# Neighbourhood attention: values for four heads side by side instead of two, loaded four heads at a time

## The chip, the cores and the metric

One core of a Trainium2 chip runs the whole kernel in one launch. The metric is the device time in microseconds (us) of one execution. The core has TensorE (PE in the profile, its weight loads PEld), VectorE (DVE), ScalarE (ACT), GpSimd (POOL) and SyncE (SP). SP and POOL also issue the DMA transfers of this kernel.

## The reference, cut to what matters

The kernel computes one layer of a hybrid backbone: 512 latent tokens (8 rows of a 64-column grid) and 256 context tokens, width 1024, float32. Only the neighbourhood attention changes. It has 16 heads of dimension 32; every query attends to an 8 x 16 window of the grid and to all 256 context tokens:

```python
def one_row(r):
    ...
    s_lat = jnp.einsum("bqhd,bkhd->bhqk", qb, kb, preferred_element_type=jnp.float32) * scale + bias
    s_lat = jnp.where(band_mask, s_lat, -jnp.inf)
    s_ctx = jnp.einsum("bqhd,bkhd->bhqk", qb, k_ctx, preferred_element_type=jnp.float32) * scale
    p = jax.nn.softmax(jnp.concatenate([s_lat, s_ctx], -1), -1).astype(v.dtype)
    n_lat = kh * GRID_W
    return (jnp.einsum("bhqk,bkhd->bqhd", p[..., :n_lat], vb)
            + jnp.einsum("bhqk,bkhd->bqhd", p[..., n_lat:], v_ctx))
```

Around it: one input projection, a gated position-mixing branch, the merge of both branches, an output projection, and a mixture of 64 experts whose weights (1 MB a tile) fill the second half of the run.

## The kernel before

**Stages, in order of time.** Normalisation and projections (to about 225 us), the first half of the gating branch (`phase_u`), then a stage that weaves two streams: `up_a` and `gates` are projections with 512-column matmuls (tile `mmp`, lines 135 to 137, three matmuls for one float32 product), and `na()` is the neighbourhood attention, advanced by `weave` some 1.5 steps after each half of a weight piece. Then `up_b`, `w_out`, the router, and the experts.

**The attention.** A unit is one head on one quarter g of the grid's columns: 128 queries against 256 latent keys (the quarter's 32-column window of all 8 rows) and 256 context keys. With 16 heads and 4 quarters that makes the 64 units that `units` lists. The tiles `q4` and `k4` hold the operands of a pair of heads `hp`; `hh` is a head's place among four. Each unit is a chain over the engines: two score matmuls (`stp`, L836 and L837), minimum and bias on DVE (L840, L841), two exponentials on ACT (L844, L845), the normalisation on DVE (L869 to L871, which completes `npr`), four transposes on PE (`tpp`, L874), and a copy to `npt` (L876, on DVE and ACT by turns).

**The products with the values** (`pvp`, L859) follow a few units later. The stationary operand is a slab of values of one head, 128 keys x 32 columns of the tile `vw`, so a matmul fills 32 of the array's 128 columns and writes 32 partitions of the PSUM tile `pv`; the moving operand is `npt` (128 columns). Heads that write different groups of 32 partitions use different columns of the array. Before, two heads are worked at a time: for each of 4 slabs of keys, one matmul for each of the two heads. In the trace each such float32 matmul is two instructions, so a batch of 2 heads x 4 slabs is 16 of them.

**Loads.** `fetch` reads a pair's `q4` and `k4` with 8 DMAs on POOL's queue (L790); two buffers each. `na_start` reads all values of all heads into one `vw` tile with 34 DMAs (L802, L804) before the first unit. `nab` reads the bias of one pair and one type of quarter on SP's queue, into the four buffers of the tag `bc`. Weight pieces (`raw`, L124) and, later, expert weights (`rw`, L1215) are also on SP's queue.

**Order.** In this stage a scheduler sets the order on each engine from the program's order and its own costs; an engine then runs its instructions strictly in that order.

Of the kernel before, what the change touches and what calls it, by code (L numbers as in the profile page):

```python
# [7 lines left out]
F32 = mybir.dt.float32  # L8
F32R = mybir.dt.float32r
# [8 lines left out]
P = 128  # L18
D = 1024
S = 512  # L20
C = 256
T = S + C
# [5 lines left out]
GBASE = (0, 8, 24, 32)  # L28
GTYPE = (0, 1, 1, 2)
# [62 lines left out]
class Kern:  # L92
# [49 lines left out]
    def run(self):  # L142
        tc, nc, A = self.tc, self.nc, self.A
        with ExitStack() as es:
# [25 lines left out]
            self.zn = zn_.__enter__()  # L170
            na = self.na()
            next(na)
            self.phase_u()
            self.weave(self.stream(self.up_a() + self.gates(0) + self.gates(1)), na, self.WV, 68)
            zn_.__exit__(None, None, None)
            mid_ = tc.tile_pool(name="mid", bufs=1, side="right", reuse_waits="tile")
# [606 lines left out]
    def na_loads(self, hp):  # L783

        nc, zn = self.nc, self.zn
        q4 = zn.tile([P, 2, S], F32R, name="q4", tag="q4", bufs=2)
        k4 = zn.tile([P, 2, T], F32R, name="k4", tag="k4", bufs=2)
        for gi in range(4):
            for t, src, part, n in ((q4, self.qdr, gi // 2, S), (k4, self.kdr, gi % 2, T)):
                nc.gpsimd.dma_start(t[gi * 32:gi * 32 + 32], src[part, hp * 64:hp * 64 + 64, :]  # L790
                                    .rearrange("(h d) t -> d h t", d=32))
        return q4, k4

    def na_start(self):
        nc, zn = self.nc, self.zn
        self.vw = zn.tile([P, 10, 512], F32, name="vw")
        v = self.vdr
        for g in range(4):
            for c in range(2):
                for r in range(4):  # L800
                    t0 = (4 * c + r) * 64 + GBASE[g]
                    nc.gpsimd.dma_start(self.vw[r * 32:r * 32 + 32, g * 2 + c, :], v[t0:t0 + 32, 64:576])  # L802
        for c in range(2):
            nc.gpsimd.dma_start(self.vw[:, 8 + c, :], v[S + c * P:S + c * P + P, 64:576])  # L804
        self.obhi, self.oblo = [], []

    def na(self):

        nc, zn = self.nc, self.zn
        units = [(hp, g, hh) for hp in range(8) for g in range(4) for hh in (hp % 2 * 2, hp % 2 * 2 + 1)]  # L810
        qk, bias, pr, pts = {}, {}, {}, {}

        def fetch(hp):
            if hp < 8:
                qk[hp] = self.na_loads(hp)

        def nab(i):
            if i < 24:
                hp = i // 3
                bias[i] = self.p1.tile([P, 2, 256], F32, name="nab", tag="bc", bufs=4)  # L820
                nc.sync.dma_start(bias[i], self.A["nab"][i % 3, hp // 2, :, hp % 2 * 512:hp % 2 * 512 + 512]
                                  .rearrange("p (h k) -> p h k", h=2))

        fetch(0), fetch(1)
        self.na_start()
        yield
        nab(0), nab(1)
        for n in range(len(units) + 4):
            if n < len(units):
                hp, g, hh = units[n]  # L830
                q4, k4 = qk[hp]
                bt = bias[hp * 3 + GTYPE[g]]
                ps = self.st_tile()
                q = q4[:, hh % 2, g * P:g * P + P]
                kw = k4[:, hh % 2, :S].rearrange("p (r c) -> p r c", c=64)[:, :, GBASE[g]:GBASE[g] + 32]
                nc.tensor.matmul(ps[:, 256:], lhsT=q, rhs=k4[:, hh % 2, S:], start=True, stop=True)  # L836
                nc.tensor.matmul(ps[:, :256], lhsT=q, rhs=kw, start=True, stop=True)  # L837
                m = zn.tile([P, 8], F32, name="nm", tag="nm", bufs=4)
                sb = zn.tile([P, 256], F32, name="nsb", tag="nsb", bufs=2)
                nc.vector.tensor_reduce(out=m[:, 0:1], in_=ps[:, 256:], axis=AX.X, op=ALU.min)  # L840
                nc.vector.tensor_tensor_reduce(out=sb, in0=ps[:, :256], in1=bt[:, hh % 2, :], scale=-1.0,  # L841
                                               scalar=m[:, 0:1], op0=ALU.add, op1=ALU.min, accum_out=m[:, 1:2])
                pr[n] = zn.tile([P, 512], F32, name="npr", tag="npr", bufs=2), m
                nc.scalar.activation(pr[n][0][:, :256], sb, AF.Exp, bias=m[:, 1:2], scale=-1.0, accum_out=m[:, 2:3])  # L844
                nc.scalar.activation(pr[n][0][:, 256:], ps[:, 256:], AF.Exp, bias=m[:, 1:2], scale=-1.0, accum_out=m[:, 3:4])  # L845
                if hh % 2 and g != 1:
                    nab(hp * 3 + GTYPE[g] + 2)
                if hh % 2 and g == 3:
                    fetch(hp + 2)
            yield  # L850
            if n >= 3 and n % 2 and n - 3 < len(units):
                hp, g, hh = units[n - 3]
                if hh + g == 0:
                    pv = self.pv_tile()
                for c in range(4):
                    vi = g * 2 + c if c < 2 else 6 + c
                    for i in range(2):
                        h = hp * 2 + i
                        nc.tensor.matmul(pv[(hh + i) * 32:(hh + i) * 32 + 32, g * P:g * P + P],  # L859
                                         lhsT=self.vw[:, vi, h * 32:h * 32 + 32],  # L860
                                         rhs=pts[n - 3 + i][:, c * P:c * P + P], start=c == 0, stop=c == 3)
                for i in range(2):
                    pts.pop(n - 3 + i)
                if hp % 2 and g == 3:
                    self.na_done(pv)
            if 0 < n <= len(units):
                hh = units[n - 1][2]
                p, m = pr.pop(n - 1)
                nc.vector.tensor_tensor(m[:, 4:5], m[:, 2:3], m[:, 3:4], op=ALU.add)  # L869
                nc.vector.reciprocal(m[:, 5:6], m[:, 4:5])  # L870
                nc.vector.tensor_scalar(p, p, m[:, 5:6], None, op0=ALU.mult)  # L871
                tp = self.tp_tile()
                for i in range(4):
                    nc.tensor.transpose(tp[:, i * P:i * P + P], p[:, i * P:i * P + P], self.ident)  # L874
                pt = zn.tile([P, 512], F32, name="npt", tag="npt", bufs=5)
                (nc.scalar.copy if hh % 2 else nc.vector.tensor_copy)(pt, tp)  # L876
                pts[n - 1] = pt
# [877 lines left out]
```

## Time and profile before

| what | value |
|---|---|
| time, median of 3 runs | 1319.64 us (1318.62 to 1322.22) |
| the profiled execution's own time | 1315.69 us |
| its span, first to last instruction | 1313.8 us |
| PE busy | 1199.2 us (91%) |
| PE weight loads busy | 835.5 us (64%) |
| DVE busy | 831.2 us (63%) |
| ACT busy | 612.5 us (47%) |
| POOL busy | 397.7 us (30%) |

Matmuls are pipelined: the profile gives a matmul its whole passage through the array, so a busy PE says that something was always in the array, not that it took work at its best rate. What a matmul costs its successors is the distance from its start to the start of the next one. Attention runs from about 285 to 495 us of the span.

### The profile page before, as it was taken

What the parts mean: (1) busy time and instruction counts of PE and PEld (TensorE: products, weight loads), DVE (VectorE), ACT (ScalarE), POOL (GpSimd) and SP (SyncE); (2) the same over time, 40 slices, a digit from 0 to 9 for tenths busy, and PEclk for the clock granted to TensorE, in tenths of its full rate; (3) what the DMA queues carried; (4) which work ended last, traced back from release to release, by engine and by line L of the source; (5) the groups of instructions that cost most, each with busy time, mean ns of one, the idle gap of its engine ahead of it and who ended that gap; (6) DMA issues with size and microseconds to landing.
All of it is one profiled execution on the core that took longest, in us unless ns stands there. A gap on an engine that the chain in (4) does not pass through costs nothing.

```text
span 1313.8 us, 18428 instructions
## 1 busy us (share of the span) xinstructions
PE 1199.2 (91%) x6305; PEld 835.5 (64%) x6305; DVE 831.2 (63%) x1470; ACT 612.5 (47%) x1086; POOL 397.7 (30%) x380
## 2 busy tenths in 40 slices
PE   6999999999999999989899899888797898898990
PEld 4875787887777778877643445655464565555660
DVE  4535356756777765675944635767676876766763
ACT  4411155345555554334523434565465566665641
POOL 2400111511211100042644534534253434443422
PEclk8999999999999999988999999989798999999996
DMA  9999553944674636584899999999999999999984
GB/s 326 323 308 296 161 175 86 224 148 113 143 163 113 151 113 214 182 320 159 265 309 365 305 355 366 349 344 332 348 358 359 347 367 363 364 376 363 365 297 145
DMA packets 107465, 353.46 MB, mean 269 GB/s; under 512 B 14081, under 2 KB 41322, under 8 KB 82410
## 3 DMA queue, kind: packets, MB, share of 16 engines
q1 hardware_dynamic: 82634, 289.86, 61.6%
q0 software_dynamic: 24272, 60.82, 19.5%
q10 hardware_dynamic: 464, 1.59, 0.3%
q8 instruction: 51, 0.84, 0.3%
q14 instruction: 44, 0.36, 0.1%
HBM read 323.45 MB, written 39.53 MB: 276 GB/s over the span
## 4 chain that ended last, share of the span: by engine, by line
DMA 30%; PE 15%; DVE 5%; issue 3%; ACT 1%; POOL 1%; SPq 0%; POOLq 0%; DVEq 0%; ACTq 0%
DMA rw<-in_w_exp_dram 27%; PE py L1340 5%; PE pg L1294 5%; DVE gq L1267 2%; PE pg L1281 2%; PE xt L1387 1%; DMA accb<-y,rows 1%; DMA xg<-h2d,half 1%; DMA accd<-y,ix 1%; DVE oh L1180 1%; PE mmp L137 1%; DMA accb<-y,ix 1%; ACT gq L1265 1%; PE mmp L136 1%; PE mmp L135 1%
## 5 line engine op out<-in xcount | busy, mean ns | idle before, releaser
L1294 PE MATMUL pg<-gq,xx 128*128 128x512 f32 x1136 | 331.6, 428 | 0.8 <-DVE gq L1267 0.8
L1267 DVE TENSOR_TENSOR gq<-rw,gq 128x1024 fp32r<-128x1024 f32 x210 | 264.1, 1270 | 82.5 <-ACT gq L1265 81.4
L1294 PEld LDWEIGHTS pg<-gq,xx 128*128 128x128 f32 x1136 | 207.0, 192 | 78.7 <-issue 30.2
L1265 ACT CAST gq<-rw 128x1024 fp32r<-128x1024 f32 x216 | 222.0, 1047 | 64.7 <-DMA rw<-in_w_exp_dram 42.1
L1340 PE MATMUL py<-rw,hT 128*128 128x512 f32 (+1 forms) x560 | 216.9, 625 | 37.2 <-DMA rw<-in_w_exp_dram 30.0
L1353 POOL TENSOR_TENSOR y<-y,gf 128x512 f32<-128x512 f32 x52 | 75.1, 1445 | 270.6 <-ACT y L1352 270.5
L1340 PEld LDWEIGHTS py<-rw,hT 128*128 128x128 f32 (+1 forms) x560 | 74.7, 171 | 125.0 <-issue 109.5
L118 ACT CAST whi<-raw 128x1024 fp32r<-128x1024 f32 (+1 forms) x60 | 61.2, 1022 | 130.8 <-PE mmp L136 38.9
L119 DVE TENSOR_TENSOR wlo<-raw,whi 128x1024 fp32r<-128x1024 f32 (+1 forms) x60 | 71.3, 1189 | 75.8 <-ACT whi L118 75.8
L135 PE MATMUL mmp<-hhi,whi 128*128 128x512 f32 x256 | 103.8, 405 | 0.0
L137 PE MATMUL mmp<-hhi,wlo 128*128 128x512 f32 x256 | 101.0, 396 | 0.0
L136 PE MATMUL mmp<-hlo,whi 128*128 128x512 f32 x256 | 100.7, 393 | 0.0
L119 DVE TENSOR_TENSOR xx<-xt,xx 128x512 fp32r<-128x512 f32 x88 | 60.2, 685 | 30.4 <-ACT xx L118 29.7
L1355 DVE SCALAR_TENSOR_TENSOR y<-py,tw,gf 128x512 f32<-128x512 f32 x52 | 38.9, 747 | 63.5 <-PE py L1340 38.8
L1375 POOL DMA_INDIRECT xg<-h2d,ix x50 | 55.4, 1107 | 76.8 <-PE xt L1387 45.7
L1387 PE MATMUL xt<-ident,xg 128*128 128x128 f32 x400 | 61.4, 277 | 7.3 <-DMA xg<-h2d,half 7.3
L790 POOL DMA_DIRECT2D q<-qdr x32 | 17.7, 553 | 147.8 <-PE stp L837 142.8
L1387 PEld LDWEIGHTS xt<-ident,xg 128*128 128x128 f32 x400 | 49.2, 143 | 20.6 <-issue 13.2
L118 ACT CAST xx<-xt 128x512 fp32r<-128x512 f32 x88 | 51.4, 585 | 16.3 <-PE xt L1387 15.4
L1362 POOL DMA_INDIRECT accb<-y,ix x31 | 54.2, 1748 | 13.0 <-POOL y L1353 7.6
L135 PEld LDWEIGHTS mmp<-hhi,whi 128*128 128x128 f32 x256 | 48.2, 188 | 12.5 <-issue 3.0
L137 PEld LDWEIGHTS mmp<-hhi,wlo 128*128 128x128 f32 x256 | 48.1, 188 | 10.7 <-issue 0.8
(426 smaller groups left out, 2199.9 us busy)
## 6 DMA issues: line engine op xcount, KB each, us to landing
rw<-in_w_exp_dram SPq DMA_DIRECT2D x195, 1024.0 KB
raw<-in_w_in_dram SPq DMA_DIRECT2D x40, 512.0 KB
araw<-in_w_ada_dram SPq DMA_DIRECT2D x64, 256.0 KB
araw<-in_w_ada_dram SPq DMA_DIRECT2D x16, 512.0 KB
k<-kdr POOLq DMA_DIRECT2D x32, 192.0 KB
nab<-in_nab_dram SPq DMA_DIRECT2D x24, 256.0 KB
x<-in_x_dram SPq DMA_DIRECT2D x8, 512.0 KB
q<-qdr POOLq DMA_DIRECT2D x32, 128.0 KB
```

The costliest lines, as they stand in the source:

```text
L118: self.nc.scalar.copy(hi, src)
L119: (eng or self.nc.vector).tensor_tensor(lo, src, self.r32(hi), op=ALU.subtract)
L135: mm(ps, lhsT=ahi, rhs=bhi, start=first, stop=False)
L136: mm(ps, lhsT=ahi, rhs=blo, start=False, stop=False)
L137: mm(ps, lhsT=alo, rhs=bhi, start=False, stop=last)
L1265: nc.scalar.copy(t[:, 0, :, sl], src)
L1267: eng.tensor_tensor(t[:, 1, :, sl], src, self.r32(t[:, 0, :, sl]), op=ALU.subtract)
L1294: nc.tensor.matmul(pg, lhsT=st.x[:, q * 2 + k, a, :], rhs=t[:, b, k, :], start=q + k + n == 0, stop=q + k + n == 3 + len(terms))
L1340: nc.tensor.matmul(py[s], lhsT=st.hT[:, j, s], rhs=d[:, j * D + c * 512:j * D + c * 512 + 512], start=j == 0, stop=j == 1)
L1353: nc.gpsimd.tensor_tensor(o, o, gf, op=ALU.mult)
L1375: nc.gpsimd.indirect_dma_start(out=st.xg[i * (P // 2):i * (P // 2) + cap], out_offset=None, in_=self.h2d[:], in_offset=bass.IndirectOffset ...
L1387: self.nc.tensor.transpose(tp[:, k * P:k * P + P], st.xg[:, (q * 4 + k) * P:(q * 4 + k + 1) * P], self.ident)
```

## The change

The units are listed by fours: for each group `two` of four heads (two pairs) and each quarter, four units, one for each head. The products with the values wait for all four, and for each slab of keys four matmuls go to the four groups of 32 columns. Values come with `na_values`, 17 DMAs for each group of four heads, into a tile of 128 columns instead of 512, with two buffers; the first two groups are read before the first unit, the third and fourth when an earlier group's products are done. `q4` and `k4` get a third buffer, three pairs are fetched ahead, and the bias tiles are ordered by the new units and read four ahead instead of two.

```diff
--- before.py
+++ after.py
@@ -783,31 +783,33 @@
     def na_loads(self, hp):
 
         nc, zn = self.nc, self.zn
-        q4 = zn.tile([P, 2, S], F32R, name="q4", tag="q4", bufs=2)
-        k4 = zn.tile([P, 2, T], F32R, name="k4", tag="k4", bufs=2)
+        q4 = zn.tile([P, 2, S], F32R, name="q4", tag="q4", bufs=3)
+        k4 = zn.tile([P, 2, T], F32R, name="k4", tag="k4", bufs=3)
         for gi in range(4):
             for t, src, part, n in ((q4, self.qdr, gi // 2, S), (k4, self.kdr, gi % 2, T)):
                 nc.gpsimd.dma_start(t[gi * 32:gi * 32 + 32], src[part, hp * 64:hp * 64 + 64, :]
                                     .rearrange("(h d) t -> d h t", d=32))
         return q4, k4
 
-    def na_start(self):
+    def na_values(self, two):
+
+        nc, v = self.nc, self.vdr
+        if two < 4:
+            t = self.vw[two] = self.zn.tile([P, 10, P], F32, name="vw", tag="vw", bufs=2)
+            cols = slice(64 + two * P, 64 + two * P + P)
+            for g in range(4):
+                for r in range(4):
+                    nc.gpsimd.dma_start(t[r * 32:r * 32 + 32, g * 2:g * 2 + 2, :],
+                                        v[:S].rearrange("(c r q) d -> r q c d", c=2, r=4)[r, GBASE[g]:GBASE[g] + 32, :, cols])
+            nc.gpsimd.dma_start(t[:, 8:], v[S:].rearrange("(c p) d -> p c d", c=2)[:, :, cols])
+
+    def na(self):
+
+
+
+
         nc, zn = self.nc, self.zn
-        self.vw = zn.tile([P, 10, 512], F32, name="vw")
-        v = self.vdr
-        for g in range(4):
-            for c in range(2):
-                for r in range(4):
-                    t0 = (4 * c + r) * 64 + GBASE[g]
-                    nc.gpsimd.dma_start(self.vw[r * 32:r * 32 + 32, g * 2 + c, :], v[t0:t0 + 32, 64:576])
-        for c in range(2):
-            nc.gpsimd.dma_start(self.vw[:, 8 + c, :], v[S + c * P:S + c * P + P, 64:576])
-        self.obhi, self.oblo = [], []
-
-    def na(self):
-
-        nc, zn = self.nc, self.zn
-        units = [(hp, g, hh) for hp in range(8) for g in range(4) for hh in (hp % 2 * 2, hp % 2 * 2 + 1)]
+        units = [(two * 2 + hh // 2, g, hh) for two in range(4) for g in range(4) for hh in range(4)]
         qk, bias, pr, pts = {}, {}, {}, {}
 
         def fetch(hp):
@@ -816,20 +818,25 @@
 
         def nab(i):
             if i < 24:
-                hp = i // 3
+                hp, ty = i // 6 * 2 + i % 2, i % 6 // 2
                 bias[i] = self.p1.tile([P, 2, 256], F32, name="nab", tag="bc", bufs=4)
-                nc.sync.dma_start(bias[i], self.A["nab"][i % 3, hp // 2, :, hp % 2 * 512:hp % 2 * 512 + 512]
+                nc.sync.dma_start(bias[i], self.A["nab"][ty, hp // 2, :, hp % 2 * 512:hp % 2 * 512 + 512]
                                   .rearrange("p (h k) -> p h k", h=2))
 
+        self.obhi, self.oblo, self.vw = [], [], {}
         fetch(0), fetch(1)
-        self.na_start()
+        self.na_values(0)
+        fetch(2)
+        self.na_values(1)
         yield
-        nab(0), nab(1)
+        for i in range(4):
+            nab(i)
         for n in range(len(units) + 4):
             if n < len(units):
                 hp, g, hh = units[n]
                 q4, k4 = qk[hp]
-                bt = bias[hp * 3 + GTYPE[g]]
+                ib = hp // 2 * 6 + GTYPE[g] * 2 + hp % 2
+                bt = bias[ib]
                 ps = self.st_tile()
                 q = q4[:, hh % 2, g * P:g * P + P]
                 kw = k4[:, hh % 2, :S].rearrange("p (r c) -> p r c", c=64)[:, :, GBASE[g]:GBASE[g] + 32]
@@ -844,25 +851,26 @@
                 nc.scalar.activation(pr[n][0][:, :256], sb, AF.Exp, bias=m[:, 1:2], scale=-1.0, accum_out=m[:, 2:3])
                 nc.scalar.activation(pr[n][0][:, 256:], ps[:, 256:], AF.Exp, bias=m[:, 1:2], scale=-1.0, accum_out=m[:, 3:4])
                 if hh % 2 and g != 1:
-                    nab(hp * 3 + GTYPE[g] + 2)
+                    nab(ib + 4)
                 if hh % 2 and g == 3:
-                    fetch(hp + 2)
+                    fetch(hp + 3)
             yield
-            if n >= 3 and n % 2 and n - 3 < len(units):
-                hp, g, hh = units[n - 3]
-                if hh + g == 0:
+            if n >= 5 and n % 4 == 1:
+                four = units[n - 5:n - 1]
+                g = four[0][1]
+                if g == 0:
                     pv = self.pv_tile()
                 for c in range(4):
                     vi = g * 2 + c if c < 2 else 6 + c
-                    for i in range(2):
-                        h = hp * 2 + i
-                        nc.tensor.matmul(pv[(hh + i) * 32:(hh + i) * 32 + 32, g * P:g * P + P],
-                                         lhsT=self.vw[:, vi, h * 32:h * 32 + 32],
-                                         rhs=pts[n - 3 + i][:, c * P:c * P + P], start=c == 0, stop=c == 3)
-                for i in range(2):
-                    pts.pop(n - 3 + i)
-                if hp % 2 and g == 3:
+                    for i, (hp, _, hh) in enumerate(four):
+                        nc.tensor.matmul(pv[hh * 32:hh * 32 + 32, g * P:g * P + P],
+                                         lhsT=self.vw[hp // 2][:, vi, hh * 32:hh * 32 + 32],
+                                         rhs=pts[n - 5 + i][:, c * P:c * P + P], start=c == 0, stop=c == 3)
+                for i in range(4):
+                    pts.pop(n - 5 + i)
+                if g == 3:
                     self.na_done(pv)
+                    self.na_values(hp // 2 + 2)
             if 0 < n <= len(units):
                 hh = units[n - 1][2]
                 p, m = pr.pop(n - 1)
```

How this moves instructions is seen at two places.

On PE, at the first products with the values (early in the stage; `stp` are score matmuls, `tpp` transposes, `mmp` the projection woven in), the row before was:

```order
L874 MATMUL tpp<-ident,npr 128x128 x4
L137 MATMUL mmp<-oahi,wlo 128x512
L859 MATMUL pvp<-npt,vw 32x128
L836 MATMUL stp<-k_2212,q_2211 128x256
L837 MATMUL stp<-k_2212,q_2211 128x256
L135 MATMUL mmp<-oahi,whi 128x512
L136 MATMUL mmp<-oalo,whi 128x512
L137 MATMUL mmp<-oahi,wlo 128x512
L859 MATMUL pvp<-npt,vw 32x128 x7
L874 MATMUL tpp<-ident,npr 128x128 x4
```

and it is now:

```order
L866 MATMUL pvp<-npt,vw 32x128 x3
L135 MATMUL mmp<-oahi,whi 128x512
L843 MATMUL stp<-k_2222,q_2221 128x256
L844 MATMUL stp<-k_2222,q_2221 128x256
L136 MATMUL mmp<-oalo,whi 128x512
L882 MATMUL tpp<-ident,npr 128x128 x4
L137 MATMUL mmp<-oahi,wlo 128x512
L135 MATMUL mmp<-oahi,whi 128x512
L136 MATMUL mmp<-oalo,whi 128x512
L137 MATMUL mmp<-oahi,wlo 128x512
L866 MATMUL pvp<-npt,vw 32x128 x13
L882 MATMUL tpp<-ident,npr 128x128 x4
```

What was a run of 1 and a run of 7 matmuls, twice for four heads, has become a run of 3 and a run of 13, once for four heads. Over the whole stage the 32 batches before stand as 48 runs (16 of 8, 16 of 7, 16 of 1), the 16 batches now as 28 (6 of 16, 10 of 13, 8 of 3, 2 of 2, 2 of 1). The 516 projection matmuls, 128 score matmuls and 256 transposes between the stage's first score and its last product are the same in number; after the last product the order on every engine is the one of before.

On POOL, the queue from the last loads of the first pairs (`q`, `k`) to the next fetch was:

```order
L790 DMA q_2221<-qdr 32x2x512
L790 DMA k_2222<-kdr 32x2x768
L802 DMA vw<-vdr 32x512 x32
L804 DMA vw<-vdr 128x512 x2
L790 DMA q_2920<-qdr 32x2x512
L790 DMA k_2921<-kdr 32x2x768
```

and it now goes on after the first pairs with the values of the first four heads, the third pair, and the values of the next four:

```order
L802 DMA vw<-vdr 32x2x128 x16
L804 DMA vw<-vdr 128x2x128
L790 DMA q_3145<-qdr 32x2x512
L790 DMA k_3146<-kdr 32x2x768
L790 DMA q_3145<-qdr 32x2x512
L790 DMA k_3146<-kdr 32x2x768
L790 DMA q_3145<-qdr 32x2x512
L790 DMA k_3146<-kdr 32x2x768
L790 DMA q_3145<-qdr 32x2x512
L790 DMA k_3146<-kdr 32x2x768
L790 DMA q_3231<-qdr 32x2x512
L790 DMA k_3232<-kdr 32x2x768
```

A load of values has moved behind the fetches of two more pairs, and there are 68 such loads in place of 34, each row of them 512 bytes instead of 2 KB.

## Rows read from the trace of the kernel before

**Rows 1.** The page: span, and busy time of each engine.

```profile
span 1313.8 us, 18428 instructions
PE 1199.2 (91%) x6305; PEld 835.5 (64%) x6305; DVE 831.2 (63%) x1470; ACT 612.5 (47%) x1086; POOL 397.7 (30%) x380
```

**Rows 2.** Busy time by stage: start:end, length, engines, granted clock, DMA share, GB/s.

```profile
core 0: us, PE busy (x) PEld busy (x) DVE busy (x) ACT busy (x) POOL busy (x), PEclk, DMA share, GB/s
225.00:285.00 60.00, 60.00 (x298) 50.74 (x297) 40.27 (x52) 20.34 (x27) 27.77 (x52) 1.00 0.75 190
285.00:495.00 210.00, 210.00 (x1421) 164.07 (x1420) 152.57 (x455) 119.89 (x336) 27.16 (x50) 1.00 0.54 132
495.00:560.00 65.00, 65.00 (x288) 53.67 (x287) 40.82 (x67) 23.85 (x44) 1.05 (x2) 1.00 0.60 201
...
690.00:1290.00 600.00, 532.08 (x2312) 321.59 (x2308) 389.28 (x479) 317.81 (x445) 243.19 (x168) 0.96 0.99 347
```

**Rows 3.** Waits of PE's weight loads, 285 to 495 us: total, times, longest.

```profile
PEld pvp L859 <- issue: 9.9, 30, 0.4
PEld tpp L874 <- issue: 5.5, 27, 0.3
PEld tpp L874 <- DVE npt L876: 1.9, 7, 0.3
...
PEld pvp L859 <- ACT npt L876: 1.7, 5, 0.4
```

**Rows 4.** SP's queue in time order: the first expert weights (start, us, instruction).

```profile
493.88 2.25 SPq L1215 DMA_DIRECT2D rw<-in_w_exp_dram  x2
...
541.09 18.36 SPq L1215 DMA_DIRECT2D rw<-in_w_exp_dram  x4
```

**Rows 5.** What SP waited for, 240 to 620 us, and POOL over the run.

```profile
SPq L1215 <- PE mmp L137: 35.2, 4, 15.9
...
POOL tri L1057 <- PE pvp L859: 53.1, 1, 53.1
```

**Rows 6.** PE in time order around a whole batch of products (start, us, instruction).

```profile
422.40 0.39 PE L136 MATMUL mmp<-hlo,whi 128*128 128x512 f32 x1
422.62 0.39 PE L137 MATMUL mmp<-hhi,wlo 128*128 128x512 f32 x1
422.94 1.07 PE L859 MATMUL pvp<-npt,vw 128*32 128x128 f32 x16
423.94 0.66 PE L874 MATMUL tpp<-ident,npr 128*128 128x128 f32 x4
```

**Rows 7.** PE in time order around a run of one product.

```profile
432.82 0.28 PE L836 MATMUL stp<-k,q 128*128 128x256 f32 x1
432.93 0.28 PE L837 MATMUL stp<-k,q 128*128 128x256 f32 x1
433.15 0.41 PE L859 MATMUL pvp<-npt,vw 128*32 128x128 f32 x2
433.48 0.50 PE L135 MATMUL mmp<-hhi,whi 128*128 128x512 f32 x1
```

**Rows 8.** PE in time order around a run of seven products.

```profile
296.29 0.40 PE L137 MATMUL mmp<-oahi,wlo 128*128 128x512 f32 x1
296.62 1.06 PE L859 MATMUL pvp<-npt,vw 128*32 128x128 f32 x14
297.61 0.66 PE L874 MATMUL tpp<-ident,npr 128*128 128x128 f32 x4
```

**Rows 9.** All products: nanoseconds minimum/median/maximum, first and last start.

```profile
L859 PEld LDWEIGHTS pvp<-npt,vw x512: 106/110/110, 295.2 to 492.8; 128*32 128x32 f32 x171
L859 PE MATMUL pvp<-npt,vw x512: 272/273/298, 295.2 to 492.9; 128*32 128x128 f32 x171
```

**Rows 10.** PE, earlier: line 223, 32-column stationary tiles on four column groups.

```profile
92.28 1.07 PE L223 MATMUL pvp<-araw,sil 128*32 128x256 f32 x16
```

**Rows 11.** POOL's queue: first and last load of values, one fetch of a pair.

```profile
244.28 0.52 POOL L802 DMA_DIRECT2D vw<-vdr  x1
...
267.71 1.11 POOL L804 DMA_DIRECT2D vw<-vdr  x2
...
433.51 0.53 POOL L790 DMA_DIRECT2D q<-qdr  x1 [22.95 <-PE stp L837]
...
439.84 0.53 POOL L790 DMA_DIRECT2D k<-kdr  x1
```

**Rows 12.** POOL's DMA queue, 433.5 to 440 and 440 to 447 us: packets, MB, share of 16 engines.

```profile
q0 software_dynamic: 343, 0.70, 51.7%
...
q0 software_dynamic: 297, 0.61, 56.0%
```

**Rows 13.** DVE: two normalisations that complete `npr`; PE: the second one's transposes.

```profile
423.18 0.48 DVE L871 TENSOR_SCALAR npr<-npr,nm 128x512 f32<-128x512 f32 x1
...
428.23 0.49 DVE L871 TENSOR_SCALAR npr<-npr,nm 128x512 f32<-128x512 f32 x1
...
430.08 0.60 PE L874 MATMUL tpp<-ident,npr 128*128 128x128 f32 x4
```

**Rows 14.** SP, a weight piece; ACT, the three splits that follow it.

```profile
427.96 0.38 SPq L124 DMA_DIRECT2D raw<-in_w_in_dram  x1
...
433.99 1.04 ACT L118 CAST whi<-raw 128x1024 fp32r<-128x1024 f32 x1
...
441.61 1.05 ACT L118 CAST whi<-raw 128x1024 fp32r<-128x1024 f32 x1 [1.91 <-PE mmp L136]
...
453.28 1.03 ACT L118 CAST whi<-raw 128x1024 fp32r<-128x1024 f32 x1
```

## Prediction

> **What bounds the kernel now.** I read the page first, then busy times by stage, then PE's waits in the stage of the change, then PE's instructions in time order. The page has PE busy for 1199.2 of 1313.8 us [rows 1], an average over stages with different limits, so the stages are told apart. From 285 to 495 us, where the attention runs, PE is busy for 210.0 of 210 us, DVE for 152.6 and ACT for 119.9; the granted clock is 1.00, the upper of its two levels (2.4 GHz), and DMA has a share of 0.54 [rows 2]. PE's own waits there are small: the two largest are "issue" at the products and at the transposes, 9.9 and 5.5 us, a few tenths each time, and those on the copies of `npt` come to 1.9 and 1.7 us [rows 3]. So the stage lasts as long as PE's list of instructions takes, and a reader should look for what each costs its successor, not for a wait.
>
> What follows hangs on PE too. From 495 to 560 PE is busy for all 65 us [rows 2]. The experts, from 690 on, are bound by DMA (share 0.99), but this stream starts when PE lets it: SP issues the first two expert tiles at 493.88, as the last product frees their memory (POOL, too, waits for that product), and goes on at 541.09 [rows 4], after waits for projection matmuls that come to 35.2 us in all [rows 5]. The order behind the last product is unchanged. Time saved in the stage therefore moves everything behind it, and I count it in full.
>
> **The products, run by run.** A run is a stretch of products with no other PE work between. Projection matmuls start 0.22 to 0.23 us apart; after the one at 422.62 the next would start at 422.85, but a run of 8 products (16 instructions) stands there, and the transposes behind it start at 423.94: the run costs 1.09 us [rows 6]. A run of 7 costs the same, 296.29 + 0.23 to 297.61 [rows 8]. A run of one product (2 instructions), after a score matmul at 432.93 with a slot of 0.11, costs 433.04 to 433.48, 0.44 us [rows 7]. Between 2 and 16 instructions lie 0.65 us. If the two heads' instructions go side by side, these are 2 and 8 steps, so a step is 0.65 / 6 = 0.108 us, and 0.22 us is what entering and leaving a run costs. 0.108 fits the 0.106 to 0.110 us of a weight load [rows 9]. A run of 7 is three pairs and one alone, two instructions each, so 8 steps as well. Before: 16 runs of 8 at 1.09, 16 of 7 at 1.09 and 16 of one at 0.44 are 41.9 us.
>
> After, 28 runs. With four heads side by side a run of 16 products is four fours, 8 steps; one of 13 is three fours and one alone, 8 steps; runs of 3, 2 and 1 are 2 steps. I add 0.01 us for the third and fourth start. That is 16 x 1.10 + 12 x 0.44 = 22.9 us, and **19.0 us saved**: 14.7 by 136 fewer steps (152 instead of 288), the rest by 20 fewer entries and exits.
>
> Four side by side on 128 columns isn't in the trace, so the step has two ends. The nearest row speaks for the lower: line 223 has 16 instructions on four groups of 32 columns, and with 256 moving columns each they take 1.07 us from the first start to the last end [rows 10], as long as 16 with 128 columns on two groups [rows 6]. Twice the columns in the same time is what four at once instead of two would give. At the other end only two ever go together: runs of 16, 13, 3, 2 and 1 then have 16, 14, 4, 2 and 2 steps, 1.95, 1.73, 0.65, 0.44 and 0.44 us, in all 6 x 1.95 + 10 x 1.73 + 8 x 0.65 + 4 x 0.44 = 36.0 us, and 5.9 us are saved. I take the first end, because line 223 is the same kind of instruction; a gain of more steps is excluded, since a weight load of 0.11 us stands in each.
>
> The Trainium skill ("TensorE: Matmul & The Clock Gate", Part 3: Packing small matmuls, The mechanism) says that weight loads overlap with matmuls under way only when they differ in row group. All of these use all 128 rows, so by that rule the loads alone would take 512 x 0.11 = 56 us, before and after, and side by side would bring nothing. The trace doesn't agree for two column groups: the runs before cost 41.9 us, loads included [rows 6 to 8].
>
> **What PE's lead was worth.** The saved time also takes lead from DVE and ACT. One unit's `npr` is complete at 423.66 and its transposes start at 423.94 [rows 6, 13], a lead of 0.28 us; another's at 428.72 and 430.08 [rows 13], a lead of 1.36. PE now gains 19.0 / 16 = 1.2 us at each batch of four units. A transposition behind it with the long lead doesn't notice; one with the short lead waits 0.9 us. If all 16 had the short lead, 14.7 us would go back; if none, nothing. I take **4 us**, about one in four, because waits on copies are few now [rows 3] and DVE has room: 152.6 us of work in a stage of 195 is 78%.
>
> **Edits that I cost at nothing.** Before the first unit POOL issues 58 loads instead of 50. The values' loads go from 244.28 to 268.8, half a microsecond each [rows 11]; eight more at 0.53 are 4 us. The first product is at 295.2 [rows 9] and now needs only the first 17 of the 34: cover is over 20 us, and beyond it each microsecond would delay the stage by one. The 34 later loads of values run on POOL's queue while POOL is busy for 27 of 210 us [rows 2]; each group of four heads' values is asked for about 20 units (60 us) before its first product. Their 512-byte rows are four times as many; what they take beyond the same bytes lies in a DMA share of 0.54. The bias tiles come four ahead instead of two, but each waits on SP's queue for the last use of its buffer, and weight pieces are queued behind it. A piece is issued at 427.96, and two splits of earlier pieces (433.99, 441.61) come before its own at 453.28 [rows 14]: 25 us of cover, of which the next bias wait may take some 10. The third buffer of `q4` and `k4` takes the memory that `vw` gives back.
>
> The tightest cover is that of the odd pairs. The fetch of pairs 3, 5 and 7 waits for the score matmul of unit 13 of a group of 16, and unit 18 reads it. In between PE's new order has 52 projections, 24 transposes, 10 score matmuls and one batch in one or two runs: 52 x 0.23 + 24 x 0.108 + 10 x 0.12 + 1.5 = 17.3 us. A fetch now is issued from 433.51 to 439.84 [rows 11], and its 1.28 MB have all passed by 447, 0.70 and 0.61 MB of its queue in the two stretches [rows 12]: at most 13.5 us. I count no wait, with 4 us to spare.
>
> **Sum.** 1315.69 (the profiled execution) - 19.0 + 4 = 1300.7 us. The median of the runs shown is 1319.64, 3.95 above that execution, so I expect **1304.6 us**.
>
> **Rivals.**
> - *The stage is given back to DVE and ACT.* Most batches meet a short lead: 8 to 15 us go back, 1308.6 to 1315.6 us. For it: leads of 0.28 us exist [rows 13]. Against it: PE's waits on these engines are under 4 us now [rows 3]. Chance 0.13.
> - *Only two columns go together.* 5.9 us saved, hardly any lead lost: about 1314 us. Against it: line 223 [rows 10]. Chance 0.06.
> - *Nothing goes together that didn't before, and only 20 entries and exits are saved*: 4.4 us, 1315.2 us. Against it: the same rows. Chance 0.02. (The Trainium skill's rule on row groups, above, would lead here.)
> - *No change.* All of the gain turns into waits, or the experts' stream starts no earlier: 1316 to 1323 us. Against it: the waits of SP for PE [rows 5]. Chance 0.05.
> - *Slower: a fetch comes late.* Unit 18's score matmul waits on PE three times, for what the fetch takes beyond 17.3 us. It turns the gain of 15 into a loss beyond 17.3 + 15 / 3 = 22.3 us, and at 30 us the time is 1304.6 + 3 x 12.7 = 1343. For it: POOL's queue now carries values too, and a fetch shares DMA with weight pieces. Against it: 13.5 us at most, and the values stand behind the fetches in the queue. Chance 0.04.
>
> **How the numbers follow.** The forecast has 0.70; its own range is a gain of 11 to 21 us, 1299 to 1309. To leave out no more than 2 in 10 I reach from 1298 to 1313, which adds two thirds of the first rival and little of the second. A change of 0.3% (4 us) is about what a measurement of this kernel can tell from none, so faster means below 1315.7: 0.70 + 0.13 + 0.06 + half of 0.02 gives 0.90; within 0.3% 0.06; slower 0.04.
>
> **What would show it.** Right: runs of 32 instructions at line 866 whose successor starts 1.1 us later than without them; products that begin near 295 us and end near 478; the first two expert tiles at about 479 on SP, and the experts' stretch as long as before. Wrong: runs of 32 that take 2 us (four don't go together); PE waits on `npr` and `npt` of over 8 us (lead lost); PE waiting on a DMA of `k` or `q` at units 18, 34 and 50 (late fetch); a first expert tile that is earlier with an end that isn't (gain lost in the experts).

## The result and the profile after

The change took the median from 1319.13 us (4 runs) to **1298.98 us** (1295.77 to 1304.4, 4 runs): a ratio of 0.9863, 95% interval 0.9834 to 0.9892, or 18 us saved with 4 us either way (the medians of these few runs lie 20 us apart). The forecast was 1304.6 us, in a range of 1298 to 1313.

The page of the changed kernel, its span and busy times:

```profile
span 1296.5 us, 18444 instructions
PE 1179.1 (91%) x6305; PEld 818.7 (63%) x6305; DVE 830.7 (64%) x1470; ACT 613.1 (47%) x1086; POOL 421.7 (33%) x414
```

No engine got less to do: the counts of PE, DVE and ACT are those of [rows 1], and POOL has 34 loads more. PE is busy for 20.1 us less, at the same share of a span that is 17.3 us shorter. By stage (columns as in [rows 2], cut where the attention ends now):

```profile
225.00:285.00 60.00, 60.00 (x299) 50.77 (x299) 40.01 (x53) 20.46 (x28) 33.56 (x60) 1.00 0.84 194
285.00:474.40 189.40, 189.28 (x1412) 149.13 (x1411) 150.39 (x452) 119.45 (x336) 41.61 (x76) 1.00 0.59 145
474.40:540.00 65.60, 65.60 (x291) 54.14 (x290) 41.43 (x70) 24.01 (x45) 0.84 (x2) 1.00 0.59 197
```

The attention takes 189.4 us, and PE is still busy for nearly all of it. (The last row is a stretch of chosen length; how long the stage behind takes is seen from SP below.) The work of DVE and ACT in the stage hasn't changed (150 and 119 us); it fills 79% and 63% of a shorter stage. PE in time order shows where the time came from: a run of six instructions, one of 26 and one of 32.

```profile
297.94 0.40 PE L137 MATMUL mmp<-oahi,wlo 128*128 128x512 f32 x1
298.27 0.42 PE L866 MATMUL pvp<-npt,vw 128*32 128x128 f32 x6
298.62 0.50 PE L135 MATMUL mmp<-oahi,whi 128*128 128x512 f32 x1
...
300.55 0.40 PE L137 MATMUL mmp<-oahi,wlo 128*128 128x512 f32 x1
300.88 1.06 PE L866 MATMUL pvp<-npt,vw 128*32 128x128 f32 x26
301.87 0.66 PE L882 MATMUL tpp<-ident,npr 128*128 128x128 f32 x4
...
450.64 0.39 PE L137 MATMUL mmp<-hhi,wlo 128*128 128x512 f32 x1
450.96 1.08 PE L866 MATMUL pvp<-npt,vw 128*32 128x128 f32 x32
451.97 0.66 PE L882 MATMUL tpp<-ident,npr 128*128 128x128 f32 x4
```

With 0.23 us taken off for the projection, the 32 instructions cost 450.64 + 0.23 to 451.97, 1.10 us: what 16 cost before [rows 6]. The 26 cost 1.09 and the six 0.45. Over the stage the 28 runs cost 22.9 us by the starts of their neighbours, where the 48 runs before cost 41.9. The step is unchanged, too, seen from one instruction:

```profile
L866 PEld LDWEIGHTS pvp<-npt,vw x512: 106/110/110, 298.3 to 473.4; 128*32 128x32 f32 x171
L866 PE MATMUL pvp<-npt,vw x512: 272/273/297, 298.3 to 473.5; 128*32 128x128 f32 x171
```

Each load and each matmul takes what it took [rows 9]; only how many go together has changed. Then the end of the stage, seen from SP's queue (first expert tiles) and from SP's waits:

```profile
474.38 0.80 SPq L1223 DMA_DIRECT2D rw<-in_w_exp_dram  x2
...
521.61 1.88 SPq L1223 DMA_DIRECT2D rw<-in_w_exp_dram  x2
```

```profile
SPq L1223 <- PE mmp L137: 35.3, 4, 15.9
```

Both marks come 19.5 us earlier than in [rows 4], so the stretch between them is as long as it was, 47.2 us, and SP waits for PE as before [rows 5]. Last, the waits of PE's weight loads from 285 to 480 us:

```profile
PEld tpp L882 <- issue: 4.0, 18, 0.4
PEld pvp L866 <- issue: 3.9, 12, 0.4
PEld pvp L866 <- ACT npt L884: 2.7, 8, 0.4
PEld tpp L882 <- ACT npt L884: 1.5, 5, 0.4
...
PEld tpp L882 <- DVE npt L884: 1.4, 5, 0.3
```

The waits named "issue" at the products fell from 9.9 to 3.9 us [rows 3], with the fewer entries. Those on the copies to `npt` rose, from 1.7 to 2.7 us at the products, and none is longer than 0.4 us. All waits that name `npt` or `npr` together are 7.5 us, against 4.5 before (the prediction's sign of a lost lead was over 8); what they cost the stage is worked out under the lead, below. PE waits for no DMA.

### The profile page after: what moved, and what is told of

It reads as the page before. It is cut to its first block, busy times and chain, and to the rows that moved or that the text cites. A ratio compares the mean times of both kernels' runs of the same rounds, so it can differ in the third digit from the quotient of the medians.

```text
span 1296.5 us, 18444 instructions
## 1 busy us (share of the span) xinstructions
PE 1179.1 (91%) x6305; PEld 818.7 (63%) x6305; DVE 830.7 (64%) x1470; ACT 613.1 (47%) x1086; POOL 421.7 (33%) x414
## 3 DMA queue, kind: packets, MB, share of 16 engines
q0 software_dynamic: 25328, 60.82, 19.9%
## 4 chain that ended last, share of the span: by engine, by line
PE 52%; DMA 30%; DVE 9%; issue 5%; ACT 2%; POOL 1%; SPq 1%; POOLq 0%; ACTq 0%; DVEq 0%
DMA rw<-in_w_exp_dram 25%; PE mmp L135 9%; PE mmp L137 9%; PE mmp L136 9%; PE py L1348 6%; PE pg L1302 5%; DVE gq L1275 3%; PE tpp L882 2%; PE pg L1289 2%; PE pvp L866 2%; DVE xx L119 1%; DMA accb<-y,rows 1%; PE xt L1395 1%; DMA xg<-h2d,half 1%; DMA araw<-in_w_ada_dram 1%
## 5 line engine op out<-in xcount | busy, mean ns | idle before, releaser
L1348 PE MATMUL py<-rw,hT 128*128 128x512 f32 (+1 forms) x560 | 219.5, 627 | 39.1 <-DMA rw<-in_w_exp_dram 36.9
L1363 DVE SCALAR_TENSOR_TENSOR y<-py,tw,gf 128x512 f32<-128x512 f32 x52 | 38.9, 747 | 62.7 <-PE py L1348 31.2
L137 PEld LDWEIGHTS mmp<-hhi,wlo 128*128 128x128 f32 x256 | 48.1, 188 | 10.2 <-issue 0.6
L1188 DVE TENSOR_TENSOR oh<-iot,posm 128x512 bf16<-128x512 bf16 (+1 forms) x66 | 43.5, 678 | 16.7 <-PE ptab L1194 16.7
```

The costliest lines, as they stand in the source:

```text
L137: mm(ps, lhsT=alo, rhs=bhi, start=False, stop=last)
L1348: nc.tensor.matmul(py[s], lhsT=st.hT[:, j, s], rhs=d[:, j * D + c * 512:j * D + c * 512 + 512], start=j == 0, stop=j == 1)
```

## Experiments

Each is a variant of the changed kernel, unless it says otherwise. Ratios are to the kernel before, run on the same chip; the distance from the change is the difference of two ratios times 1319 us, and carries some 4 us of uncertainty from either.

**1. The products head by head.** All else stays: the same loads, the same order around the products.

```diff
-                for c in range(4):
-                    vi = g * 2 + c if c < 2 else 6 + c
-                    for i, (hp, _, hh) in enumerate(four):
+                for i, (hp, _, hh) in enumerate(four):
+                    for c in range(4):
+                        vi = g * 2 + c if c < 2 else 6 + c
```

> The changed kernel with the products of a batch in another order: all four slabs of one head, then those of the next, so that neighbours in the queue use the same 32 columns of the array. Loads, bias, unit order and the number of products stay. If the gain is four column groups working at once (a step of 0.108 us, 0.22 us to enter and leave a run), the 16 batches have about 29 to 32 steps each and 26 runs: 56 to 61 us in place of 22.9, the attention stage is 33 to 38 us longer, and the time is about 1332 to 1337 us. If the gain came from the loads, the bias order or fewer runs, nothing changes: about 1299 us.

Measured: 1321.85 us (10 runs), ratio 1.0035 (1.0017 to 1.0054), 22.7 us above the change. The products cost 44.9 us, 22.0 more, and the first expert tile is issued at 496.70, 22.3 us later. So the products decide, almost microsecond for microsecond. The expected size was missed, 56 to 61 us of products and 1332 to 1337 in all, because the run of 32 isn't 32 steps long:

```profile
314.23 0.39 PE L137 MATMUL mmp<-oahi,wlo 128*128 128x512 f32 x1
314.54 2.46 PE L866 MATMUL pvp<-npt,vw 128*32 128x128 f32 x32
316.94 0.66 PE L882 MATMUL tpp<-ident,npr 128*128 128x128 f32 x4
```

It costs 2.48 us, about 21 steps. The single records show why: four instructions start alone, 0.11 us apart, then they start in twos (315.004 and 315.010, 315.113 and 315.143), and the last four are alone again. Shorter runs agree: 2, 4, 6 and 8 instructions cost 0.43, 0.64, 0.86 and 1.08 us, a step each, and every further eight add 0.47 us, about four steps (16 cost 1.55, 24 cost 2.02). That is as if each head's first four start beside the last four of the head before, 8 + 3 x 4 = 20 steps. The records don't name the head, so this reading is an inference from the spacing.

**2. Two heads at a time**, with the new units, loads and waits.

```diff
-                for c in range(4):
-                    vi = g * 2 + c if c < 2 else 6 + c
-                    for i, (hp, _, hh) in enumerate(four):
+                for i0 in (0, 2):
+                  for c in range(4):
+                    vi = g * 2 + c if c < 2 else 6 + c
+                    for i, (hp, _, hh) in list(enumerate(four))[i0:i0 + 2]:
```

> The changed kernel with each batch worked as two pairs of heads, one behind the other in the same run, so that two column groups work at once instead of four. By the step of 0.108 us the batches have 16 steps instead of 8, in 25 runs: about 33 us in place of 22.9, the stage 10 us longer, the time about 1309 us. If what counts is the number of runs (25 here, 28 in the changed kernel, 48 before), the time stays at 1299 us or just under.

Measured: 1308.74 us, ratio 0.9925 (0.9895 to 0.9954), 8 us above the change. Products 31.2 us, 8.3 more, a run of 32 at 1.57 us; first expert tile 10.2 us later, of which 2.2 lie in a first score matmul that is later.

```profile
314.65 0.40 PE L137 MATMUL mmp<-oahi,wlo 128*128 128x512 f32 x1
314.97 1.54 PE L867 MATMUL pvp<-npt,vw 128*32 128x128 f32 x32
316.44 0.66 PE L883 MATMUL tpp<-ident,npr 128*128 128x128 f32 x4
```

The time is the expected one, the run isn't: 16 steps would be 1.95 us. The second pair adds 0.48 us to the 1.09 of the first, four to five steps instead of eight, and in the middle of the run the records start in fours (315.434 to 315.453). So two against four is isolated only in part. The order inside the batches is worth 8.3 us of the products; the other 10.7 us of their saving come with joining the batches, about 5 of them by 23 fewer runs at 0.22 us.

**3. The old products** (two heads, asked for as soon as two are ready), with the new loads and the new order of units.

```diff
-            if n >= 5 and n % 4 == 1:
-                four = units[n - 5:n - 1]
+            if n >= 3 and n % 2 and n - 3 < len(units):
+                pair = units[n - 3:n - 1]
```

> The changed kernel with the products of before: two heads in a batch, every second unit, and all other edits kept (unit order, values four heads at a time, third buffer, bias four ahead). If the products carry the whole gain, their 51 runs cost about 43 us and the time is that of the kernel before, 1319 us (1316 to 1322). If the other edits carry part of it, the time is under 1313 us; if they cost something that the products hide, over 1323 us.

Measured: 1321.48 us (10 runs), ratio 1.0027 (1.0009 to 1.0045), 21.6 us above the change. Products 43.2 us in 51 runs, first expert tile 494.91. The other edits bring nothing by themselves; 1.3 us of the small loss are the three more runs. The rest, some 2 us, lies within the interval of the ratio, and the trace doesn't have it in the stage: from the first score matmul to the first expert tile it is 210.57 us, 1.7 more than the 208.92 before.

**4. The products one step later**, so that nothing waits for the fourth head's copy.

```diff
-            if n >= 5 and n % 4 == 1:
-                four = units[n - 5:n - 1]
+            if n >= 6 and n % 4 == 2:
+                four = units[n - 6:n - 2]
```

> The changed kernel with each batch of products one step later, when the fourth head's copy is older; the same five buffers for the copies. The order then has 22 runs, 13 of them whole. By 0.22 us a run and 0.108 a step they cost about 20 us in place of 22.9, so the time falls by 2 to 4 us to 1295 to 1297 us. If the later batch holds up the copy that needs its buffer, and PE waits for that copy's unit, the gain is lost and the time is 1299 to 1303 us.

Measured: 1299.06 us (6 runs), ratio 0.9866 (0.984 to 0.9892). Products 20.4 us in 22 runs, 2.4 less; the first expert tile is issued at 474.33, the same moment as with the change. That mark misleads here: the scheduler now has 12 more projections in front of the last product (528 instead of 516) and 12 fewer behind it. From the first score matmul to the last projection with `hhi` PE carries out the same set of instructions in the change and in this variant. That projection, with the change and then here:

```profile
484.56 0.39 PE L137 MATMUL mmp<-hhi,wlo 128*128 128x512 f32 x1
```

```profile
481.74 0.39 PE L137 MATMUL mmp<-hhi,wlo 128*128 128x512 f32 x1
```

Counted from the first score matmul (284.29 and 284.04) these are 200.27 and 197.70 us, 2.6 less, and the second mark on SP is 2.9 us earlier (518.73). So the saving arrives in the stage. The expected 1295 to 1297 us are missed by the median, but 2.4 us are less than these times can tell apart, and a version that beats the change isn't shown. The rival's 1299 us came without the rival's reason, a gain lost to a late copy.

**5. Two buffers of `q4` and `k4` instead of three**, the tightest place of the prediction.

```diff
-        q4 = zn.tile([P, 2, S], F32R, name="q4", tag="q4", bufs=3)
-        k4 = zn.tile([P, 2, T], F32R, name="k4", tag="k4", bufs=3)
+        q4 = zn.tile([P, 2, S], F32R, name="q4", tag="q4", bufs=2)
+        k4 = zn.tile([P, 2, T], F32R, name="k4", tag="k4", bufs=2)
...
-        fetch(2)
...
-                    fetch(hp + 3)
+                    fetch(hp + 2)
```

> The new kernel with two buffers of q4 and k4 instead of three (the first two pairs are read before the first unit, each later pair when the one two before it is used up). In the program's order 59 projection matmuls now stand on PE between the last score matmul that reads a pair (units 13, 29, 45) and the first that needs the next one, and 110 before the second next (17 and 28 us at 0.226 us a projection and the like), so a fetch of some 13 us is still covered; the products with the values stand in 51 runs (30 of 2 instructions, 14 of 26, 2 of 32, the rest small), and by the prediction's prices they cost 16 x 1.09 + 35 x 0.44 = 32.9 us instead of 22.9. Theory A (the fetch is covered, only the products cost): 1299 + 10 = 1309 us, with no wait of PE for q or k over 2 us. Theory B (the third buffer is what keeps the units evenly spread): the three gaps of about 33 us hold 5 units each, the other 49 units have to pass in the remaining 90 us at 2.4 us of DVE work each, 117 us, so the stage gets some 26 us longer besides: 1320 to 1340 us, slower than before the change, and PE waits on DVE and ACT grow by 20 us or more. Theory C (the fetch comes late, the rival that was to make the change slower): PE waits on q and k of 3 x 5 us or more.

Measured: 1328.02 us (8 runs), ratio 1.0076 (1.0046 to 1.0106), 28 us above the change. In size that is theory B, and PE waits for no DMA of `q` or `k`, so C falls. Where the time goes, two stretches of the stage show:

```profile
285.00:485.00 200.00, 199.99 (x1282) 152.74 (x1281) 126.69 (x365) 106.70 (x284) 44.86 (x82) 1.00 0.59 138
485.00:517.00 32.00, 21.00 (x181) 13.92 (x180) 26.28 (x90) 17.89 (x61) 0.62 (x2) 0.93 0.32 109
```

Up to 485 us PE has no gap. The last projection in front of the last product starts at 485.54; by then 600 have been done since the first score, where the change has 516 by its last product. Those that the scheduler put in front of the late pairs are missing at the end. From there PE is busy for 21 of 32 us, and its time order shows units with nothing between them:

```profile
503.80 0.38 PE L842 MATMUL stp<-k,q 128*128 128x256 f32 x1
504.02 0.28 PE L843 MATMUL stp<-k,q 128*128 128x256 f32 x1
505.24 0.39 PE L842 MATMUL stp<-k,q 128*128 128x256 f32 x1 [0.94 <-ACT npr L851]
505.46 0.28 PE L843 MATMUL stp<-k,q 128*128 128x256 f32 x1
505.67 0.41 PE L865 MATMUL pvp<-npt,vw 128*32 128x128 f32 x2
506.08 0.63 PE L881 MATMUL tpp<-ident,npr 128*128 128x128 f32 x4
507.38 1.06 PE L865 MATMUL pvp<-npt,vw 128*32 128x128 f32 x26 [0.68 <-ACT npt L883]
```

Theory B had the loss spread over all units between the gaps; it lies in one piece at the end, where eleven units pass at the pace of their chains. Another part is the products, split into 51 runs, 10 us by the expectation's prices. A third part is the clock. From 485 to 511 us PE was busy for some 18 of 26 us; from 512.50 to 522.80 the granted clock is 0.50, the lower level (1.2 GHz), and the last run of 26 takes 1.91 us where it took 1.06 before the fall:

```profile
512.50:522.80 10.30, 7.88 (x44) 5.45 (x45) 2.45 (x8) 1.73 (x6) 1.10 (x2) 0.50 0.70 207
```

```profile
517.05 1.91 PE L865 MATMUL pvp<-npt,vw 128*32 128x128 f32 x26 [0.68 <-ACT npt L883]
```

How the 28 us divide between the three wasn't measured.

**6. Bias tiles two ahead** instead of four.

```diff
-        for i in range(4):
+        for i in range(2):
             nab(i)
...
-                    nab(ib + 4)
+                    nab(ib + 2)
```

> The new kernel with the bias tiles read two ahead again instead of four (two before the first unit); PE's order of products is the same. The kernel with the old products and the other edits came out some 3 us slower than before, 1.3 us of which were its runs of products. If the earlier bias tiles are the rest (a wait on SP's queue with weight pieces behind it), 1296 to 1297.5 us; if they cost nothing, 1299 us within 1.5, and PE's waits in the stage as in the new kernel.

Measured: 1299.87 us, ratio 0.9872 (0.9826 to 0.9918); products 22.9 us, first expert tile 474.55, waits of PE as with the change. The time alone can't tell 2 us (its interval is 6 us either way); the trace can: from the first score matmul to the first expert tile it is 189.81 us against 190.09 with the change. The bias tiles cost the stage nothing, as costed.

**7 and 8. One more VectorE operation in each unit's chain**, in the changed kernel and in the one before. It multiplies by 1.

```diff
                 nc.vector.tensor_scalar(p, p, m[:, 5:6], None, op0=ALU.mult)
+                nc.vector.tensor_scalar(p, p, 1.0, None, op0=ALU.mult)
```

> The new kernel with one more VectorE operation of about 0.48 us in each unit's chain, between the normalisation and the transposes (a multiplication by 1), 64 of them, 31 us of VectorE work in a stage of 189 us where it had about 152. The products fall into 38 runs (16 long, 22 short), 27.1 us instead of 22.9. If PE's lead still covers the chain, the time grows by the products alone: 1299 + 4 = 1303 us (up to 1306 with a few short waits). If the change used up the lead, each of the 64 units' transposes waits up to 0.5 us longer: up to 1299 + 4 + 31 = 1334 us; in between, say 1315, if VectorE with 183 us of work becomes the bound in stretches.

> The kernel before with the same additional VectorE operation. Its products fall into 57 runs (32 whole, 25 of one product) instead of 48, 45.9 us instead of 41.9. With a stage of 208 us for 183 us of VectorE work the lead should cover it: 1319 + 4 = 1323 us, up to 1327. If the lead that the change took is worth much, the additional operation costs the new kernel clearly more than this one (by 5 us or more); if it is worth nothing, both pay about 4 us.

Measured: in the changed kernel 1307.26 us (8 runs), ratio 0.9933 (0.99 to 0.9965), 9.2 us above the change; in the one before 1322.22 us (10 runs), ratio 1.0052 (1.0029 to 1.0074), 6.9 us above it. The operation itself, in the changed kernel (DVE, 285 to 483 us: busy time, mean ns):

```profile
L880 DVE TENSOR_SCALAR npr<-npr 128x512 f32<-128x512 f32 x64 | 27.3, 427 | 0.4
```

The first expert tiles come at 483.30 and 499.75, 8.9 and 5.9 us later than without it. As in experiment 4 this mark misleads: the last product has 16 more projections in front of it in the one (532) and 5 more in the other (521). The last projection with `hhi`, in the changed kernel with the operation, then in the kernel before without it and with it:

```profile
489.90 0.39 PE L137 MATMUL mmp<-hhi,wlo 128*128 128x512 f32 x1
```

```profile
503.97 0.39 PE L137 MATMUL mmp<-hhi,wlo 128*128 128x512 f32 x1
```

```profile
508.72 0.39 PE L137 MATMUL mmp<-hhi,wlo 128*128 128x512 f32 x1
```

From the first score matmul (283.62, 284.96 and 284.00) it is 206.28 us against 200.27 in the changed kernel and 224.72 against 219.01 in the one before, 6.0 and 5.7 us more. Of this the products, in more runs, are 27.2 - 22.9 = 4.3 and 45.8 - 41.9 = 3.9 us. So the chain itself cost the stage 1.7 us of the 27.3 added in the one and 1.8 in the other: nearly all of the delay disappears in PE's lead, after the change as before it. The times, 9.2 and 6.9 us, lie between the expectation's two cases, and their difference is less than they can tell apart.

## Why the prediction was right

**The bound.** PE's order sets the stage, and the saving goes through to the experts: shown by experiments 1 to 3, where 22.0, 8.3 and 20.3 us more in the products are 22.7, 8.2 and 21.6 us more in the end. In the stage itself, from the first score matmul to the last projection with `hhi`, they are 21.7, 8.0 and 20.5 us more, and in experiment 4 2.4 us fewer are 2.6 fewer. The signs that the prediction asked for are there: the products run from 298.27 to 473.55 (forecast: near 295 to near 478), and the first expert tile comes at 474.38, some 4.6 us before the forecast's 479, mostly for the term of the lead below.

**The products.** Forecast 22.9 us, measured 22.9; the runs of 32, 26, six, four and two instructions at 1.10, 1.09, 0.44, 0.43 and 0.43 us (medians), a step of 0.108 with four heads side by side as with two. The rival in which only two go together would have had runs of 32 at 1.95 us. The single records show the fours: in the run at 450.96 four matmuls start from 450.957 to 450.977 and four more from 451.090 to 451.110. The rule of the Trainium skill ("TensorE: Matmul & The Clock Gate", Part 3: Packing small matmuls, The mechanism), that weight loads overlap with matmuls under way only in another row group, doesn't hold for these. In that run the fifth load starts at 450.983, while the first four matmuls, in the same 128 rows, are under way; and 512 loads of 0.11 us one after another would be 56 us, where experiment 1, experiment 2 and the change took 44.9, 31.2 and 22.9 us for all products.

**The lead, the term that was mis-sized.** The prediction gave back 4 us to DVE and ACT. In the profiled execution of before the first score matmul starts at 284.96:

```profile
284.96 0.28 PE L836 MATMUL stp<-k,q 128*128 128x256 f32 x1
```

and in that of the change at 284.29:

```profile
284.29 0.28 PE L843 MATMUL stp<-k,q 128*128 128x256 f32 x1
```

From there to the first expert tile it is 208.92 us before [rows 4] and 190.09 after, 18.8 us less; the products alone are 19.0 less. So 0.2 us went back, though the waits that name `npt` or `npr` grew by 3 us. The lead did shrink: from the end of a unit's normalisation to its transposes the median went from 1.30 to 0.73 us over the 64 units, and those under 0.3 us rose from 6 to 14. But a short lead isn't a wait. The working took a lead of 0.28 us as used up by a gain of 1.2 us, as if DVE kept its times while PE came earlier; the units' chains begin with PE's score matmuls, so DVE and ACT move forward with PE as long as they have room, and experiments 7 and 8 show that they have: the chain's delay costs the changed kernel no more than the one before.

The lead of 0.28 us itself was misread. Counted in order, the unit that is complete at 423.66 has its transposes at 425.38, a lead of 1.72 us; those at 423.94 belong to the unit before it, complete at 420.74. The copies, which go to DVE and ACT by turns, bear this out: the unit complete at 423.66 is the 44th of the 64, the second head of its pair, so its copy is ACT's, the one at 426.07. In the kernel before:

```profile
420.25 0.49 DVE L871 TENSOR_SCALAR npr<-npr,nm 128x512 f32<-128x512 f32 x1
...
424.63 0.69 DVE L876 COPY npt<-tpp 128x512 f32<-128x512 f32 x1 [0.97 <-PE tpp L874]
...
425.38 0.65 PE L874 MATMUL tpp<-ident,npr 128*128 128x128 f32 x4
426.07 0.59 ACT L876 COPY npt<-tpp 128x512 f32<-128x512 f32 x1 [2.20 <-PE tpp L874]
```

Leads that short do exist, the six of 64 above; what made the 4 us too large is the reasoning and not this unit.

The forecast's 1304.6 without that term is 1300.6, and 1298.98 was measured. How close it came is in part luck: the median lies 1 us inside the stated range, and the four runs go from 1295.77 to 1304.4.

**Behind the stage.** Both marks on SP are 19.5 us earlier, the span is 17.3 us shorter, the medians lie 20 us apart. From the second mark to the end the profiled execution lost 2.2 us (772.7 before, 774.9 after); over the profiled executions of this document, experiment 5 left out, that stretch goes from 771.3 to 781.4 us, so 2 us there can't be told from the spread.

**The edits at nothing.** Together they don't show in the time (experiment 3), nor do the bias tiles alone (experiment 6). Without the third buffer the new order loses 28 us (experiment 5). On POOL's queue the smaller rows cost little: 60.82 MB as before, with a share of 19.9% of the span (19.5% before), and 1056 packets more for the whole run. The odd pairs' cover, estimated at 17.3 us, is 18.7 to 19.2 us from score to score, and no fetch came late. (A fetch is 1.31 MB, not 1.28; the bound of 13.5 us doesn't hang on it.) The rival on the other side, a fetch that takes longer than its cover, was priced as three waits on PE. No run tested it in that form. Experiment 5 shows a neighbour of it, a fetch that the program starts later: there the scheduler fills the time in front of the late pair with projections, PE never waits for the fetch, and the bill comes at the end of the stage, where the projections are missing. A fetch that is slow only on the chip would meet an order that doesn't allow for it; what that costs stays open.

## What to carry to other kernels

Matmuls that fill 32 of 128 columns cost by the step here and not by the instruction: order them so that neighbours write four different column groups, and join their batches, since each run paid 0.22 us for itself. Before costing a saving on the bounding engine as partly given back to the engines that feed it, ask what starts their chains: if the bounding engine does, they move with it, and their share of the stage (79% here) said more than single short leads. Where a scheduler has filler work and its order allows for a load that starts late, the lateness can show as filler that is missing later, not as a wait. And a mark such as the first expert tile measures a stage only if the same work stands in front of it: count that before reading a difference from it.

## What was not expected of the hardware

With the products head by head, neighbouring instructions go to the same 32 columns, and still a run of 32 cost 2.48 us instead of the 3.7 that 32 steps and 0.22 us would be. By the spacing of the starts PE begins the next head's, on other columns, before the one at hand is through (the inference of experiment 1). Four side by side needs the right order, but the bad order cost twice the time, 44.9 us against 22.9, and not four times.

The values' rows of 512 bytes are four times as many as those of 2 KB; with the same bytes the packets on POOL's DMA queue rose by 1056, from 24272 to 25328:

```profile
q0 software_dynamic: 25328, 60.82, 19.9%
```
